# Stick-breaking attention in a two-block transformer kernel: one item per head becomes one item per pair of heads

## The chip, the cores and the metric

The kernel runs on one core of one Trainium2 chip. The metric is device time in microseconds, the median of three runs. PE is the tensor engine (matmuls; PEld are its weight loads), DVE the vector engine, ACT the scalar engine, POOL GpSimd, SP the queue that issues most of the DMAs. Each engine works through its own instructions in the order in which the program issued them.

## The reference

Two transformer blocks on 512 tokens of width 1024. The first block has two layers, and each layer mixes an attention of one kind (NSA) with stick-breaking attention; the change touches the stick-breaking attention only, so it is run twice (layer 0 and layer 1).

```python
def stick_breaking_attention(q, k, v):            # 8 heads of 64, blocks of 128
    for i in range(T // SB_QBLOCK):
        z = einsum(q[q0:q1], k[:q1]) * scale
        strict = k_pos < q_pos
        log_1m = where(strict, -softplus(z), 0.0)
        later = cumsum(log_1m, reverse=True) - log_1m
        w = where(strict, exp(log_sigmoid(z) + later), 0.0)
        out = einsum(w, v[:q1])
```

In `hybrid_mixer` the result goes on as `y = g_a * (o_nsa @ w_proj_nsa) + g_b * (o_sb @ w_proj_sb)`.

## The kernel before

**The stage.** `sb_attn` keeps keys on the partitions and queries on the free axis. An item is one head and one block `j` of 128 keys, with the `512 - 128 j` queries that may see it, so 128 to 512 columns. There are 32 items a layer. Per item:

- PE computes the scores into one PSUM bank: one fp32 matmul with 64 contracted rows (L1190), which the machine runs as two passes, and one small matmul that adds the mask (L1191). Even heads lie on partitions 0 to 63, odd heads on 64 to 127.
- DVE clips them (L1195), ACT takes the exponential and then ln(1+x) (L1196, L1197), DVE takes the maximum with the scores (L1201): this is softplus. ACT rounds it into the high part (L1202), DVE subtracts it for the low part (L1206).
- PE adds the sums over the later keys to the scores, with a matrix of minus ones over each later key block (L1214) and a triangle for the block itself (L1216), each for the high and the low part. Block 3 is padded to 256 columns with zeros.
- ACT takes the exponential, the weights (L1217). PE multiplies them by the values into an output bank (L1224; fp32 again, 64 output rows, a head's half of the partitions). After a pair's last item ACT and DVE split that bank into high and low part (L231, L232).

**The order.** It is written by hand as a software pipeline: iteration `t` computes scores of item `t`, softplus of `t` and `t-1`, the sums and the weights of `t-2`, and every second iteration the outputs of `t-4` and `t-3`. `self.fill(0.6)` puts other work between: `merge_a`, the NSA projection, cut into 32 steps of three matmuls of 512 columns (L223 to L225). Eight steps use one weight unit; every four steps end in two DVE instructions (L729, L730) that empty the PSUM bank. Four banks hold scores, two hold outputs, two the filler.

**The weights.** `Weights` has four slots of a high and a low tile. ACT rounds a unit into the high tile (L112), POOL (here) or DVE subtracts for the low one (L121). `nsa_in` borrows two of the four slots for NSA's keys (`K4`), and `nsa_attn` brings them back at its end. After `sb_attn` comes `merge_out`, whose first matmuls (L223 with `Hh`) take the next PSUM bank in turn.

Of the kernel before, what the change touches and what calls it, by code (L numbers as in the profile page):

```python
# [16 lines left out]
T = 512  # L17
# [156 lines left out]
class Net:  # L174
# [633 lines left out]
    def mix1(self, l):  # L808
        tc = self.tc
        pool = lambda st, name, side: st.enter_context(tc.tile_pool(name=name, bufs=1, side=side))  # L810
        with ExitStack() as st:
            O = pool(st, "oA", "left")
            oA = (O.tile([128, 4, T], F32R, name="oAh"), O.tile([128, 4, T], F32R, name="oAl"))
            tA = O.tile([128, 8, T], F32, name="tA")
            with ExitStack() as sb:
                S = pool(sb, "sv", "right")
                sv = S.tile([128, 4, 512], F32, name="sv")
                with ExitStack() as sn:
                    NP = pool(sn, "nsa", "left")
                    qS = NP.tile([128, 8, T], F32R, name="qS")  # L820
                    vN = NP.tile([128, 4, 2, 128], F32, name="vN")
                    vc = NP.tile([128, 2, 4, 64], F32, name="vc")
                    gt = NP.tile([128, 4, 24], F32, name="gt")
                    gcm = NP.tile([128, 4, 8], F32, name="gcm")
                    kl1 = NP.tile([128, 1024], F32R, name="kl1")
                    with ExitStack() as s2:
                        K4 = self.nsa_in(l, pool(s2, "nsain", "left"), qS, vN, vc, gt, gcm, kl1, sv, tA)
                    S = pool(sb, "sqk", "right")
                    sq = S.tile([128, 4, T], F32, name="sq")
                    sk = S.tile([128, 4, T], F32, name="sk")  # L830
                    with ExitStack() as s2:
                        self.nsa_attn(pool(s2, "nsaat", "left"), qS, K4, vN, vc, gt, gcm, kl1, oA, sq, sk, tA)
                O = pool(st, "oB", "left")
                oB = (O.tile([128, 4, T], F32R, name="oBh"), O.tile([128, 4, T], F32R, name="oBl"))
                with ExitStack() as s2:
                    self.sb_attn(pool(s2, "sbat", "left"), sq, sk, sv, oB, self.merge_a(oA, tA))
            self.merge_out(st, 4, oB, tA, self.a["g_post_mix"][l], self.a["g_pre_ffn"][l])

    def nsa_in(self, l, R, qS, vN, vc, gt, gcm, kl1, sv, tA):
# [18 lines left out]
        def rope(ps, i, nh, out):  # L858
# [142 lines left out]
    def nsa_attn(self, R, qS, K4, vN, vc, gt, gcm, kl1, oA, sq, sk, tA):  # L1001
        nc, PS = self.nc, self.PS
        mm = nc.tensor.matmul
# [21 lines left out]
        items = [(i, kv * 4 + g) for i in range(4) for g in range(4) for kv in range(2)]  # L1025
        n = len(items)
# [131 lines left out]
        self.drain()  # L1158
        self.W.flush()
        self.W.defer, self.W.lo = False, nc.vector  # L1160
        self.W.bring_back()

    def sb_attn(self, R, sq, sk, sv, oB, fill):
        nc, PS = self.nc, self.PS
        mm = nc.tensor.matmul
        A = [h[:, e * T:e * T + T] for h in self.hn for e in range(2)]
        NZ = 4
        self.banks = [6, 7]
        Wt = [h[:, e * T:e * T + T] for h in (self.gpost, self.gpre) for e in range(2)]
        nb = {0: 1, 1: 2, 2: 2, 3: 2}  # L1170
        SP = {j: [R.tile([128, 2, max(256, T - 128 * j)], F32R, name=f"sp{j}_{i}") for i in range(nb[j])] for j in range(4)}
        for t in SP[3]:
            nc.vector.memset(t[:, :, 0:128].bitcast(F32), 0.0)
        items = [(0, 3), (0, 2)]
        for h in range(7):
            items += [(h, 1), (h + 1, 3), (h, 0), (h + 1, 2)]
        items += [(7, 1), (7, 0)]
        n = len(items)

        def part_of(t):  # L1180
            h, j = items[t]
            N = T - 128 * j
            o = 128 if j == 3 else 0
            return h, j, N, PS[:, t % NZ, :N], A[t % 4][:, :N], SP[j][h % nb[j]][:, :, o:o + N]

        def st_z(t):
            h, j, N, z, a, _ = part_of(t)
            p, e = divmod(h, 2)
            r = slice(64 * e, 64 * e + 64)
            mm(z, sk[r, p, j * 128:j * 128 + 128], sq[r, p, j * 128:], start=True, stop=False)  # L1190
            mm(z[:, 0:128], self.identb, self.sbmaskb, start=False, stop=True)  # L1191

        def st_exp(t):
            h, j, N, z, a, _ = part_of(t)
            nc.vector.tensor_scalar(a, z, 40.0, None, op0=OP.min)  # L1195
            nc.scalar.activation(a, a, AF.Exp)  # L1196
            nc.scalar.activation(a, a, AF.Ln, bias=1.0)  # L1197

        def st_sp(t):
            h, j, N, z, a, sp = part_of(t)  # L1200
            nc.vector.tensor_max(a, a, z)  # L1201
            nc.scalar.activation(sp[:, 0], a, AF.Copy)  # L1202

        def st_lo(t):
            h, j, N, z, a, sp = part_of(t)
            nc.vector.tensor_sub(sp[:, 1], a, sp[:, 0].bitcast(F32))  # L1206

        def st_c(t):
            h, j, N, z, _, sp = part_of(t)
            for j2 in range(3, j, -1):  # L1210
                s2 = SP[j2][h % nb[j2]]
                c0 = (min(j2, 2) - j) * 128
                for e in range(2):
                    mm(z[:, c0:], self.nones, s2[:, e], start=False, stop=False, skip_group_check=True)  # L1214
            for e in range(2):
                mm(z, self.ntri, sp[:, e], start=False, stop=e == 1, skip_group_check=True)  # L1216
            nc.scalar.activation(Wt[t % 4][:, :N], z, AF.Exp)  # L1217

        def st_e(ts):
            for t in ts:  # L1220
                h, j = items[t]
                p, e = divmod(h, 2)
                O = PS[:, NZ + p % 2, :]
                mm(O[64 * e:64 * e + 64, j * 128:], sv[:, j, h * 64:h * 64 + 64], Wt[t % 4][:, :T - 128 * j],  # L1224
                   start=j == 3, stop=j == 0, skip_group_check=True)
                if j == 0 and e == 1:
                    self.split2(oB[0][:, p], oB[1][:, p], O)
# [20 lines left out]
        self.W.defer, self.W.lo = False, nc.vector  # L1248


    def reg_mix2(self):
# [472 lines left out]
```

## Time and profile before

| | |
|---|---|
| median of three runs | 2891.37 us (2890.51 to 2892.0) |
| profiled execution | 2889.35 us, its span 2887.4 us |
| PE busy | 2832.1 us (98%) |
| DVE, ACT, POOL busy | 1416.8 us (49%), 1128.5 us (39%), 370.5 us (13%) |
| granted clock of PE, mean share of full speed | 0.994 |

Busy time is the time in which an engine has an instruction under way. Matmuls overlap in the pipeline, so a matmul's own duration is longer than what it adds: that is the distance from its start to the start of the next one.

### The profile page before, as it was taken

Reading aid. Unit: us, or ns where it says so; the run is one execution under the profiler, and the core shown is the slowest. Engines: PE = TensorE matmul, PEld = TensorE weight load, DVE = VectorE, ACT = ScalarE, POOL = GpSimd, SP = SyncE. Lnnn points to the kernel's source line nnn. Section 1 sums busy time; section 2 is a strip of 40 time slices with the busy share of each in tenths; the row PEclk is TensorE's granted clock in tenths of the full one; section 3 lists DMA queues with packets and bytes.
Section 4 is the critical chain, followed back from the end, with each engine's and each line's share of the span. In section 5 each row is a group of like instructions: output and inputs, shape, how many; then the busy total and the mean of one; then the engine's idle time right before and its main releaser. Section 6 shows DMA issues by size and latency. Waiting matters only on the chain.

```text
span 2887.4 us, 34979 instructions
## 1 busy us (share of the span) xinstructions
PE 2832.1 (98%) x14228; PEld 2290.7 (79%) x14228; DVE 1416.8 (49%) x2248; ACT 1128.5 (39%) x2046; POOL 370.5 (13%) x287
## 2 busy tenths in 40 slices
PE   8999999999999999999999999999999999999998
PEld 7777578888878786688888888888776978888887
DVE  5666645544555566545535453233653343533334
ACT  3444634433433445534424342222444232432222
POOL 5221100100122221101101020000522010000000
PEclk9999999999999999999999999999999999999999
DMA  4111123333322111132323322322331222322322
GB/s 156 63 59 30 37 95 100 109 122 93 96 97 90 59 37 45 52 131 76 110 99 99 116 88 88 101 96 95 127 98 61 77 77 95 110 88 95 102 90 78
DMA packets 234322, 255.48 MB, mean 88 GB/s; under 512 B 33073, under 2 KB 193185, under 8 KB 233777
## 3 DMA queue, kind: packets, MB, share of 16 engines
q1 hardware_dynamic: 228016, 233.53, 25.3%
q0 software_dynamic: 4992, 16.94, 1.9%
q10 hardware_dynamic: 1152, 2.77, 0.3%
q8 instruction: 111, 1.82, 0.3%
q14 instruction: 51, 0.41, 0.0%
HBM read 248.60 MB, written 5.53 MB: 88 GB/s over the span
## 4 chain that ended last, share of the span: by engine, by line
PE 92%; DVE 5%; ACT 2%; issue 1%; DMA 0%; DVEq 0%; SPq 0%; ACTq 0%
PE PS L223 25%; PE PS L225 25%; PE PS L224 25%; PE PS L422 2%; PE PS L1190 2%; DVE x L585 2%; PE PS L1124 1%; PE PS L1110 1%; PE PS L1080 1%; PE PS L425 1%; PE PS L1224 1%; PE PS L460 1%; PE PS L1214 1%; PE PS L1216 1%; DVE hn L339 1%
## 5 line engine op out<-in xcount | busy, mean ns | idle before, releaser
L121 DVE TENSOR_TENSOR wlo<-wraw,whi 128x1024 fp32r<-128x1024 f32 (+3 forms) x364 | 437.1, 1206 | 730.3 <-ACT whi L112 730.2
L223 PE MATMUL PS<-Hh,whi 128*128 128x512 f32 x1952 | 776.1, 398 | 1.2 <-DVE nak L1358 0.2
L225 PE MATMUL PS<-Hh,wlo 128*128 128x512 f32 x1952 | 761.1, 390 | 0.2 <-DVE wlo L121 0.2
L224 PE MATMUL PS<-Hl,whi 128*128 128x512 f32 x1952 | 760.5, 390 | 0.0
L112 ACT ACTIVATE whi<-wraw 128x1024 fp32r<-128x1024 f32 (+2 forms) x432 | 436.9, 1016 | 341.6 <-PE PS L225 280.5
L223 PEld LDWEIGHTS PS<-Hh,whi 128*128 128x128 f32 x1952 | 366.6, 188 | 85.2 <-issue 10.3
L225 PEld LDWEIGHTS PS<-Hh,wlo 128*128 128x128 f32 x1952 | 366.4, 188 | 78.2 <-DVE wlo L121 0.8
L224 PEld LDWEIGHTS PS<-Hl,whi 128*128 128x128 f32 x1952 | 367.0, 188 | 70.7
L121 POOL TENSOR_TENSOR wlo<-wraw,whi 128x1024 fp32r<-128x1024 f32 (+1 forms) x68 | 168.2, 2475 | 1304.5 <-ACT whi L112 1304.5
L223 PE MATMUL PS<-whi,gh 128*128 128x512 f32 x624 | 242.9, 389 | 0.0
L225 PE MATMUL PS<-whi,gl 128*128 128x512 f32 x624 | 242.8, 389 | 0.0
L224 PE MATMUL PS<-wlo,gh 128*128 128x512 f32 x624 | 242.7, 389 | 0.0
L231 ACT ACTIVATE gh<-gg 128x512 fp32r<-128x512 f32 x88 | 55.6, 632 | 327.1 <-DVE gg L643 178.9
L223 PEld LDWEIGHTS PS<-whi,gh 128*128 128x128 f32 x624 | 117.4, 188 | 24.5
L224 PEld LDWEIGHTS PS<-wlo,gh 128*128 128x128 f32 x624 | 117.3, 188 | 24.5
L225 PEld LDWEIGHTS PS<-whi,gl 128*128 128x128 f32 x624 | 117.1, 188 | 24.1
L641 POOL TENSOR_TENSOR gg<-cg,cu 128x512 f32<-128x512 f32 x44 | 56.7, 1288 | 549.5 <-DVE cu L624 549.5
L232 DVE TENSOR_TENSOR gl<-gg,gh 128x512 fp32r<-128x512 f32 x88 | 60.9, 693 | 125.5 <-ACT gh L231 125.5
L223 PE MATMUL PS<-whi,Hh 128*128 128x512 f32 (+2 forms) x320 | 118.4, 370 | 2.4 <-ACT whi L112 2.2
L224 PE MATMUL PS<-wlo,Hh 128*128 128x512 f32 (+2 forms) x320 | 116.7, 365 | 0.5 <-DVE wlo L121 0.5
L225 PE MATMUL PS<-whi,Hl 128*128 128x512 f32 (+2 forms) x320 | 116.0, 363 | 0.1
L1091 DVE TENSOR_REDUCE small<-PS 128x2 f32<-128x256 f32 (+3 forms) x64 | 52.7, 824 | 72.0 <-PE PS L1082 61.1
(340 smaller groups left out, 4082.7 us busy)
## 6 DMA issues: line engine op xcount, KB each, us to landing
wraw<-in_w_in_dram SPq DMA_DIRECT2D x56, 1024.0 KB, 5.0
wraw<-in_w_up_dram SPq DMA_DIRECT2D x40, 1024.0 KB, 5.1
wraw<-in_ffn_w_gate_dram SPq DMA_DIRECT2D x20, 1024.0 KB, 5.2
wraw<-in_ffn_w_up_dram SPq DMA_DIRECT2D x20, 1024.0 KB, 5.2
wraw<-in_w_down_dram SPq DMA_DIRECT2D x16, 1024.0 KB, 5.0
wraw<-in_ffn_w_down_dram SPq DMA_DIRECT2D x16, 1024.0 KB, 5.1
wraw<-in_w_out_dram SPq DMA_DIRECT2D x12, 1024.0 KB, 4.9
wraw<-in_w_down_dram SPq DMA_DIRECT2D x8, 768.0 KB, 4.3
```

The lines of the kernel that those rows point to most:

```text
L112: self.nc.scalar.activation(hi, raw, AF.Copy)
L121: self.lo.tensor_sub(lo, raw, hi.bitcast(F32))
L223: mm(out, lh, rh, start=start, stop=False)
L224: mm(out, lh, rl, start=False, stop=False)
L225: mm(out, ll, rh, start=False, stop=stop)
L231: nc.scalar.activation(hi, src, AF.Copy)
L232: nc.vector.tensor_sub(lo, src, hi.bitcast(F32))
L422: self.nc.tensor.matmul(ps[:, sl], ww[:, k], self.Hh[:, k, sl], start=k == 0 and ww is w[0], stop=False)
L585: nc.vector.scalar_tensor_tensor(x, f, r, x, op0=OP.mult, op1=OP.add)
L641: nc.gpsimd.tensor_mul(g, cg[j % 3], cu[j % 3])
L1091: nc.vector.reduce_max(m, S2, axis=AX.X, negate=True)
L1190: mm(z, sk[r, p, j * 128:j * 128 + 128], sq[r, p, j * 128:], start=True, stop=False)
```

## The change

An item becomes a key block of a **pair** of heads, with the two heads in two neighbouring PSUM banks, and each DVE and ACT step is one instruction over both. Key blocks 2 and 3 are one item of 256 + 128 columns, so a pair has three items (2, then 1, then 0) of 2 x 384, 2 x 384 and 2 x 512 columns, and a layer has 12 items in 15 iterations. Three items hold six banks; outputs have one bank (6), the filler one (7). The softplus of block 0, and of every second pair that of block 1, lies in the two borrowed weight slots, which come back only at the end of `sb_attn`. Within an iteration ACT now has `ln` of item `t` behind the weights of `t-2`, and outputs are made for item `t-3` in every iteration. The filler gives a fixed number of steps: four in the first two iterations, two in each later one. The padding of block 3 is gone. The first line of the diff stands at the end of `nsa_attn`.

```diff
-        self.W.bring_back()
...
-    def sb_attn(self, R, sq, sk, sv, oB, fill):
+    def sb_attn(self, R, sq, sk, sv, oB, K4, fill):
...
+        pair = lambda v: v.rearrange("p (e n) -> p e n", e=2)
+        A = [pair(h) for h in self.hn]
+        Wt = [pair(self.gpost), pair(self.gpre)]
+        K4 = [pair(t) for t in K4]
+        self.banks = [7]
+        O = PS[:, 6, :]
+        sp = lambda n, m: [R.tile([128, 2, m], F32R, name=f"{n}{e}") for e in range(2)]
+        SP = {0: [K4[0:2]] * 2, 1: [sp("spb", 384), K4[2:4]], 2: [sp(f"spa{i}", 384) for i in range(2)]}
+        items = [(p, j) for p in range(4) for j in (2, 1, 0)]
...
+            s = 2 * (t % 3)
+            return p, j, PS[:, s:s + 2, :N], A[t % 2][:, :, :N], [v[:, :, :N] for v in SP[j][p % 2]]
 
         def st_z(t):
-            h, j, N, z, a, _ = part_of(t)
-            p, e = divmod(h, 2)
-            r = slice(64 * e, 64 * e + 64)
-            mm(z, sk[r, p, j * 128:j * 128 + 128], sq[r, p, j * 128:], start=True, stop=False)
-            mm(z[:, 0:128], self.identb, self.sbmaskb, start=False, stop=True)
...
+            for jj in (2, 3) if j == 2 else (j,):
+                c = 256 if jj == 3 else 0
+                for e in range(2):
+                    r = slice(64 * e, 64 * e + 64)
+                    mm(z[:, e, c:c + T - 128 * jj], sk[r, p, jj * 128:jj * 128 + 128], sq[r, p, jj * 128:], start=c == 0, stop=False)
...
+        def st_min(t):
+            _, _, z, a, _ = part_of(t)
             nc.vector.tensor_scalar(a, z, 40.0, None, op0=OP.min)
             nc.scalar.activation(a, a, AF.Exp)
+
+        def st_ln(t):
+            a = part_of(t)[3]
             nc.scalar.activation(a, a, AF.Ln, bias=1.0)
...
+            sa, sb = SP[2][p % 2], SP[1][p % 2]
+            later(128 * (3 - j), sa, 256, 384)
+            if j < 2:
+                later(128 * (2 - j), sa, 0, 256)
+            if j == 0:
+                later(128, sb, 0, 384)
+            for i, u in enumerate(s):
+                mm(z[:, e], self.ntri, u[:, e], start=False, stop=i == 1, skip_group_check=True)
...
             if 0 <= t - 1 < n:
                 st_sp(t - 1)
             if t < n:
-                st_exp(t)
+                st_min(t)
             if 0 <= t - 1 < n:
                 st_lo(t - 1)
             if 0 <= t - 2 < n:
-                st_c(t - 2)
-            self.fill(0.6)
-            if t >= 4 and t % 2 == 0:
-                st_e((t - 4, t - 3))
+                st_c(t - 2, 0)
+                st_c(t - 2, 1)
+                st_w(t - 2)
+            if t < n:
+                st_ln(t)
+            steps(4 if t < 2 else 2)
+            if 0 <= t - 3 < n:
+                st_e(t - 3)
```

In the changed file the scores are L1192 and the masks L1195, `min` is L1199, `exp` L1200, `ln` L1204, `max` L1208, the rounding L1209, the low part L1213, ones and triangle L1220 and L1229, the weights L1233, the outputs L1241.

**PE inside the stage.** Before, in the second head's turn: outputs of two items (`gpre` holds the weights, `sv` the values), then the scores of one head (`sq`, `sk`), its mask, sums (`sp`), one filler step, and the next head's scores.

```order
L1224 MATMUL PS<-gpre,sv 64x384
L1224 MATMUL PS<-gpre,sv 64x128
L1190 MATMUL PS<-sq,sk 128x128
L1191 LDWEIGHTS identb
L1191 MATMUL PS<-sbmaskb,identb 128x128
L1214 MATMUL PS<-sp_1_2276,nones 128x256 x2
L1216 MATMUL PS<-sp_1_2274,ntri 128x256 x2
L223 MATMUL PS<-oAh,whi_66 128x512
L224 MATMUL PS<-oAl,whi_66 128x512
L225 MATMUL PS<-oAh,wlo_67 128x512
L1190 MATMUL PS<-sq,sk 128x512
```

Now, in iteration 4, the outputs of both heads, then the scores of both heads, both masks, and the first head's sums (`spa` is the softplus of blocks 2 and 3, `spb` that of block 1).

```order
L1241 MATMUL PS<-gpost,sv 64x256 x2
L1192 MATMUL PS<-sq,sk 128x384 x2
L1195 LDWEIGHTS identb
L1195 MATMUL PS<-sbmaskb,identb 128x128
L1195 LDWEIGHTS identb
L1195 MATMUL PS<-sbmaskb,identb 128x128
L1220 MATMUL PS<-spa_2272,nones 128x128
L1220 MATMUL PS<-spa_2273,nones 128x128
L1220 MATMUL PS<-spa_2272,nones 128x256
L1220 MATMUL PS<-spa_2273,nones 128x256
L1220 MATMUL PS<-spb_2270,nones 128x384
L1220 MATMUL PS<-spb_2271,nones 128x384
```

The score matmuls of the even and the odd head now stand side by side, as do the two output matmuls of equal width.

**ACT inside the stage.** Before, with `hn` the work tile and `gpre`, `gpost` the weights:

```order
L1202 ACTIVATE sp_1_2276<-hn_78 128x128
L1196 ACTIVATE hn_77<-hn_77 128x512
L1197 ACTIVATE hn_77<-hn_77 128x512
L1217 ACTIVATE gpre<-PS 128x384
L1202 ACTIVATE sp_0_2270<-hn_77 128x512
L1196 ACTIVATE hn_77<-hn_77 128x256
```

Now, from the rounding in iteration 5 to the pair's output split:

```order
L1209 ACTIVATE whi_70<-hn_77 128x2x384
L1200 ACTIVATE hn_78<-hn_78 128x1024
L1233 ACTIVATE gpre<-PS 128x2x384
L1204 ACTIVATE hn_78<-hn_78 128x1024
L231 ACTIVATE oBh<-PS 128x512
```

The `ln` has moved behind the weights of the item two before, and the split of the output bank stands behind it.

**PE at the end of the stage.** Before, with what each waits for, the last sums, the last filler step, the last outputs, and the first matmul of `merge_out` (`Hh`):

```order
L1216 MATMUL PS<-sp_0_2270,ntri 128x512 [waits DVE_49]
L223 MATMUL PS<-oAh,whi_70 128x512
L224 MATMUL PS<-oAl,whi_70 128x512
L225 MATMUL PS<-oAh,wlo_71 128x512
L1224 MATMUL PS<-gpre,sv 64x384 [waits Activation_49]
L1224 MATMUL PS<-gpre,sv 64x512 [waits Activation_49]
L223 MATMUL PS<-Hh,whi_66 128x512
```

Now:

```order
L1241 MATMUL PS<-gpost,sv 64x384 [waits Activation_49]
L1241 MATMUL PS<-gpost,sv 64x384
L1241 MATMUL PS<-gpre,sv 64x512 [waits Activation_49]
L1241 MATMUL PS<-gpre,sv 64x512
L223 MATMUL PS<-Hh,whi_66 128x512 [waits DVE_49]
L224 MATMUL PS<-Hl,whi_66 128x512
```

The first matmul of `merge_out` now waits for DVE: its bank in turn is 6, which held the outputs that DVE's L232 reads last.

## Rows read from the trace of the kernel before

**Rows 1.** Busy time by stretch: the stage in both layers.

The columns are the stretch, its length, busy time and instructions of PE, PEld, DVE, ACT and POOL, granted clock, DMA share, GB/s.

```profile
277.00:369.00 92.00, 91.08 (x419) 51.49 (x417) 60.62 (x118) 62.43 (x138) 10.56 (x5) 1.00 0.09 30
1114.00:1206.00 92.00, 91.20 (x417) 51.83 (x418) 60.70 (x119) 62.54 (x139) 11.41 (x5) 1.00 0.09 29
```

**Rows 2.** All waits of PE in layer 0's stage, 277.11 to 369.

```profile
PE PS L223 <- DVE oAl L232: 0.8, 1, 0.8
```

**Rows 3.** Timeline of PE in that stage: start, duration, instruction, count.

```profile
283.00 0.48 PE L1190 MATMUL PS<-sq,sk 64*128 64x128 f32 x2
283.42 0.23 PE L1191 MATMUL PS<-sbmaskb,identb 128*128 128x128 bf16 x1
...
284.25 0.39 PE L224 MATMUL PS<-oAl,whi 128*128 128x512 f32 x1
284.48 0.39 PE L225 MATMUL PS<-oAh,wlo 128*128 128x512 f32 x1
284.79 1.12 PE L1190 MATMUL PS<-sq,sk 64*128 64x512 f32 x2
285.85 0.23 PE L1191 MATMUL PS<-sbmaskb,identb 128*128 128x128 bf16 x1
...
288.38 0.70 PE L1190 MATMUL PS<-sq,sk 64*128 64x256 f32 x2
289.01 0.23 PE L1191 MATMUL PS<-sbmaskb,identb 128*128 128x128 bf16 x1
...
293.19 0.86 PE L1224 MATMUL PS<-gpre,sv 128*64 128x384 f32 x4
293.98 0.48 PE L1190 MATMUL PS<-sq,sk 64*128 64x128 f32 x2
...
364.16 1.07 PE L1224 MATMUL PS<-gpost,sv 128*64 128x512 f32 x4
365.16 1.09 PE L1214 MATMUL PS<-sp,nones 128*128 128x256 f32 x6
```

**Rows 4.** Timeline of PE in the second block: two heads' scores side by side.

```profile
2181.39 0.70 PE L1481 MATMUL PS<-hn,hn 64*128 64x256 f32 x4
2182.02 0.50 PE L223 MATMUL PS<-Hh,whi 128*128 128x512 f32 x1
```

**Rows 5.** Groups by line and shape, whole run: busy us, mean ns of one.

```profile
L112 ACT ACTIVATE whi<-wraw 128x1024 fp32r<-128x1024 f32 x392 | 410.0, 1050 | 282.9 <-PE PS L225 236.0 <-issue 18.9 <-DMA wraw<-in_w_in_dram 9.7
L112 ACT ACTIVATE whi<-wraw 128x768 fp32r<-128x768 f32 x8 | 6.7, 842 | 0.1
L1091 DVE TENSOR_REDUCE small<-PS 128x2 f32<-128x1024 f32 x16 | 19.6, 1225 | 24.5 <-PE PS L1082 24.5
L1091 DVE TENSOR_REDUCE small<-PS 128x2 f32<-128x768 f32 x16 | 15.3, 958 | 18.6 <-PE PS L1082 18.6
L1206 DVE TENSOR_TENSOR sp<-hn,sp 128x256 fp32r<-128x256 f32 x16 | 17.3, 1080 | 2.3 <-ACT sp L1202 2.1
```

**Rows 6.** Timeline of all engines: a hand-over, and the end of the stage.

```profile
282.13 0.56 DVE L1195 TENSOR_SCALAR hn<-PS 128x384 f32<-128x384 f32 x1
...
282.73 0.52 ACT L1196 ACTIVATE hn<-hn 128x384 f32<-128x384 f32 x1
...
368.99 0.50 PE L223 MATMUL PS<-Hh,whi 128*128 128x512 f32 x1
369.10 0.60 ACT L231 ACTIVATE oBh<-PS 128x512 fp32r<-128x512 f32 x1 [0.80 <-PE PS L1224]
...
369.73 0.69 DVE L232 TENSOR_TENSOR oBl<-PS,oBh 128x512 fp32r<-128x512 f32 x1 [1.59 <-ACT oBh L231]
```

**Rows 7.** Busy time by stretch elsewhere: PE with gaps, and its granted clock.

```profile
2254.30:2257.80 3.50, 2.93 (x21) 2.51 (x21) 2.20 (x11) 2.40 (x12) 0.00 (x0) 1.00 0.26 90
2257.80:2261.30 3.50, 3.50 (x17) 3.28 (x16) 1.85 (x11) 3.10 (x15) 0.36 (x1) 0.51 0.00 0
2330.00:2344.00 14.00, 11.08 (x78) 6.48 (x74) 9.43 (x26) 4.15 (x7) 2.04 (x2) 1.00 0.24 75
```

More of the change, by code (lines that the diff above doesn't have):

```diff
@@ L835, in mix1 @@
                 with ExitStack() as s2:
-                    self.sb_attn(pool(s2, "sbat", "left"), sq, sk, sv, oB, self.merge_a(oA, tA))
+                    self.sb_attn(pool(s2, "sbat", "left"), sq, sk, sv, oB, K4, self.merge_a(oA, tA))
             self.merge_out(st, 4, oB, tA, self.a["g_post_mix"][l], self.a["g_pre_ffn"][l])
@@ L1160, in nsa_attn @@
         self.W.defer, self.W.lo = False, nc.vector
-        self.W.bring_back()
-    def sb_attn(self, R, sq, sk, sv, oB, fill):
+    def sb_attn(self, R, sq, sk, sv, oB, K4, fill):
         nc, PS = self.nc, self.PS
         mm = nc.tensor.matmul
[L1166 to L1177, printed above, removed]
+        pair = lambda v: v.rearrange("p (e n) -> p e n", e=2)
[7 more added lines that the diff above has]
+        items = [(p, j) for p in range(4) for j in (2, 1, 0)]
@@ L1178, in sb_attn @@
         n = len(items)
+        NJ = {0: 512, 1: 384, 2: 384}
         def part_of(t):
[L1181 to L1184, printed above, removed]
+            p, j = items[t]
+            N = NJ[j]
+            s = 2 * (t % 3)
+            return p, j, PS[:, s:s + 2, :N], A[t % 2][:, :, :N], [v[:, :, :N] for v in SP[j][p % 2]]
         def st_z(t):
-            h, j, N, z, a, _ = part_of(t)
@@ L1188, in st_z @@
-            p, e = divmod(h, 2)
-            r = slice(64 * e, 64 * e + 64)
-            mm(z, sk[r, p, j * 128:j * 128 + 128], sq[r, p, j * 128:], start=True, stop=False)
-            mm(z[:, 0:128], self.identb, self.sbmaskb, start=False, stop=True)
-        def st_exp(t):
-            h, j, N, z, a, _ = part_of(t)
+            p, j, z, _, _ = part_of(t)
+            for jj in (2, 3) if j == 2 else (j,):
[3 more added lines that the diff above has]
+                    mm(z[:, e, c:c + T - 128 * jj], sk[r, p, jj * 128:jj * 128 + 128], sq[r, p, jj * 128:], start=c == 0, stop=False)
@@ L1195, in st_exp @@
+            for c in (0, 256) if j == 2 else (0,):
+                for e in range(2):
+                    mm(z[:, e, c:c + 128], self.identb, self.sbmaskb, start=False, stop=c == 256 or j < 2)
+        def st_min(t):
+            _, _, z, a, _ = part_of(t)
             nc.vector.tensor_scalar(a, z, 40.0, None, op0=OP.min)
             nc.scalar.activation(a, a, AF.Exp)
+        def st_ln(t):
+            a = part_of(t)[3]
             nc.scalar.activation(a, a, AF.Ln, bias=1.0)
         def st_sp(t):
-            h, j, N, z, a, sp = part_of(t)
+            _, _, z, a, s = part_of(t)
@@ L1201, in st_sp @@
             nc.vector.tensor_max(a, a, z)
-            nc.scalar.activation(sp[:, 0], a, AF.Copy)
+            nc.scalar.activation(s[0], a, AF.Copy)
         def st_lo(t):
[L1205 to L1212, printed above, removed]
-                for e in range(2):
[L1214 to L1227, printed above, removed]
+            _, _, _, a, s = part_of(t)
+            nc.vector.tensor_sub(s[1], a, s[0].bitcast(F32))
@@ new lines, in st_c, with later @@
+        def st_c(t, e):
+            p, j, z, _, s = part_of(t)
+            def later(c, v, c0, c1):
+                for u in v:
+                    mm(z[:, e, c:c + c1 - c0], self.nones, u[:, e, c0:c1], start=False, stop=False, skip_group_check=True)
+            sa, sb = SP[2][p % 2], SP[1][p % 2]
[6 more added lines that the diff above has]
+                mm(z[:, e], self.ntri, u[:, e], start=False, stop=i == 1, skip_group_check=True)
@@ new lines, in st_w, with st_e @@
+        def st_w(t):
+            p, j, z, _, _ = part_of(t)
+            nc.scalar.activation(Wt[t % 2][:, :, :NJ[j]], z, AF.Exp)
+        def st_e(t):
+            p, j = items[t]
+            for jj in (3, 2) if j == 2 else (j,):
+                c = 256 if jj == 3 else 0
+                for e in range(2):
+                    h = 2 * p + e
+                    mm(O[64 * e:64 * e + 64, jj * 128:], sv[:, jj, h * 64:h * 64 + 64], Wt[t % 2][:, e, c:c + T - 128 * jj],
+                       start=jj == 3, stop=jj == 0, skip_group_check=True)
+            if j == 0:
+                self.split2(oB[0][:, p], oB[1][:, p], O)
@@ L1229, in sb_attn, with steps @@
+        def steps(k):
+            self.W.flush()
+            while k and self.fillq:
+                if next(self.fillq[0], None) is None:
+                    self.fillq.pop(0)
+                else:
+                    k -= 1
         self.table(LN_EXP_SET)
@@ L1248, in sb_attn @@
         self.W.defer, self.W.lo = False, nc.vector
+        self.W.bring_back()
     def reg_mix2(self):
```

## The prediction, written before the changed kernel ran

> **What bounds the kernel now.** I read the busy times by stretch first, because the change touches only two stretches. In both the tensor engine is busy for 91.1 and 91.2 of 92 us at the full clock, while DVE and ACT are busy for about two thirds [rows 1]. The view of waits then shows that PE waits only once in layer 0's stage, 0.8 us at its start [rows 2]. So the stage is as long as the sum of PE's distances from one start to the next, and what DVE and ACT do in it is hidden. Shortening DVE or ACT work gains nothing by itself; what counts is what PE no longer streams, and then whether DVE and ACT can follow the faster PE.
>
> **What PE saves, per pair of heads.** I count distances from start to start on PE's timeline.
>
> *Scores.* One head's matmul of 128 columns takes 283.00 to 283.42, 0.42 us; of 256, 0.63; of 512, 1.06 [rows 3]. The 384 wide one lies half way between the last two, 0.84. One head costs 0.42 + 0.63 + 0.84 + 1.06 = 2.95, a pair 5.90 today. In the second block the scores of an even and an odd head already stand side by side, 256 columns each, and the four passes of both take 2181.39 to 2182.02, 0.63 us [rows 4]: as much as one head alone. The lower and the upper half of the array work at the same time. The change puts them side by side for every width, so a pair should cost 2.95 and **save 2.95**. The bounds are nothing (no overlap) and 2.95; I take the row with the same form.
>
> *Outputs.* A 384 wide matmul beside a 128 wide one takes 0.79 us, a 512 wide beside a 256 wide one 1.00 [rows 3]. A pair has two of each, 3.58. Now the two heads' matmuls have equal widths. For 512 with 512 I take 1.00, for 384 with 384 0.79, since today's time already is about that of the wider one; for the item of 128 and 256 columns no row exists, and it lies between 0.79 and 1.00: 0.89. Sum 2.68, **saved 0.90**.
>
> *Changes of the array's shape.* From the last filler matmul to the scores PE needs 0.31 us (284.48 to 284.79) against 0.23 between filler matmuls (284.25 to 284.48) [rows 3]. Eight groups of scores and four of outputs a pair become three and three: six times 0.08, **saved 0.5**.
>
> *Masks and sums.* There are eight mask matmuls a pair before and after, 0.23 long each in the pipeline [rows 3], but they now stand in runs. That may cost nothing or up to 8 x 0.23; they are short and their weights the same, so I let it lose 0.1. The sums need 36 matmuls a pair instead of 40, since the triangle covers blocks 2 and 3 at once; some get wider, six get narrower. I price this at nothing; at the most it saves 4 x 0.23 = 0.9.
>
> Together 2.95 + 0.90 + 0.5 - 0.1 = 4.25 us a pair, 17.0 us a layer. PE alone would need 92 - 17 = **75.0 us** a stage.
>
> **Whether DVE and ACT can follow.** They have fewer instructions, but each is longer, and they form a chain, because only three items are under way and each engine takes its work in order. From `ln` of item t-1: DVE takes the maximum, then clips item t while ACT rounds; ACT takes `exp` of t, the weights of t-2, `ln` of t. The prices are those of 1024 and 768 columns: ACT 1.05 and 0.84, DVE 1.23 and 0.96 [rows 5], the DVE ones being reads of PSUM like these. A hand-over costs 282.73 - (282.13 + 0.56) = 0.04 us [rows 6], about 0.2 an iteration.
>
> - Key block 2 follows block 0: 1.23 + 1.05 (rounding, longer than clipping at 0.96) + 0.84 + 0.84 + 0.84 + 0.2 = 5.0.
> - Block 1: 0.96 + 0.96 + 0.84 + 1.05 + 0.84 + 0.2 = 4.85.
> - Block 0: 0.96 + 1.23 + 1.05 + 0.84 + 1.05 + 0.2 = 5.33.
>
> That is 15.2 a pair. Once a pair the output split gets in: PE comes to the outputs only after two filler steps (6 x 0.23 = 1.4) and the outputs themselves (1.0), then ACT copies in 0.60 and DVE subtracts in 0.69 [rows 6], so DVE is free 3.7 us after the sums, where `ln` would have released it after 0.84 + 1.05 = 1.9. The next maximum is 1.8 late. Three such holds lie inside the stage. Four pairs are 60.8, the holds 5.4, and a tail follows the last `ln`: maximum 1.23, rounding 1.05, low part 1.23, the second head's nine sum matmuls (1.6 at 0.18), weights 1.05, outputs 1.0, hand-overs 0.2 = 7.4. The chain alone needs **73.6 us**.
>
> **The end of the stage.** The first matmul of `merge_out` now waits for the split of the outputs, since its bank in turn is the output bank. Before, that split ran beside it: 368.99 to 369.73 + 0.69 = 370.42 [rows 6]. This **costs 1.4 us** a layer.
>
> **What costs nothing.** With two weight slots instead of four only one unit is split ahead. The filler takes a unit every four iterations, some 20 us, and a split needs 1.05 on ACT [rows 5] and then POOL, all beside that; the first gate unit of `merge_out` (24 x 0.23 = 5.5 us) covers the second's. Uncovered it would be 1.05 and a DVE copy of 1.2, 2.3 us a layer. The DMAs are the same ones, later by a few us.
>
> **The sum.** PE alone gives 75.0, the chain alone 73.6. Two lines so equal wait for each other in turn, since scores of item t need the bank that the weights of t-3 release; I add 0.1 us for each of the 15 iterations, a choice between nothing and the 0.8 that PE's one wait had. Stage 75.0 + 1.5 + 1.4 = 78 at the most, 75.0 + 1.4 = 76.4 at the least. I take **77**, 15 us less a layer, 30 in all. The profiled execution took 2889.35 us, its span 2887.4; 30 less is 2859.4, and the median of the runs lay 2.0 above that execution: **2861 us**.
>
> **The rivals.** A change within 0.2% (5.8 us) could hardly be told from none.
>
> *DVE and ACT become the bound outright.* When POOL works on a weight unit, DVE's low parts stretch: those of 256 columns took 1080 ns on average [rows 5], where a clip of 384 columns takes 0.56 [rows 6]. POOL does five units in a stage, 11.41 / 5 = 2.3 us each [rows 1]. If each delayed the chain by its whole copy and the holds were doubled, the chain would be 73.6 + 11.5 + 5.4 = 90.5 and 1.4, with nothing saved; half of that gives 82 + 1.4 a stage, 8.6 saved, about 2874. Against it: after clipping, DVE has 2.7 us until the next maximum and needs 1.2 for the low part, so 1.5 of each stretch is free. Beside this stands the Trainium skill, TensorEngine Tiling (Array Packing), section Performance Considerations: packing speeds up TensorE but not the emptying of PSUM, which may become the bottleneck. By it the outcome is this rival. Chance of 2871 to 2885: 0.14.
>
> *The two heads' scores do not overlap.* Then 11.8 of the 17.0 go, PE needs 86.8 + 1.4, and the time is 2884 to 2888. The pairs in the second block speak against it. Chance 0.04.
>
> *Nothing that can be told,* for instance because weights come late after the stage and give the gain back: 0.03, and half of the last rival falls here too.
>
> *Slower: PE's clock falls.* PE will wait a little in every iteration. Elsewhere a stretch with PE busy for 2.93 of 3.5 us was followed by one at a granted clock of 0.51, 1.2 GHz; another with 11.08 of 14 stayed at 1.00 [rows 7]. In a stretch at half clock PE does half of its work. The 30 us are eaten up when 60 us of the two stages, of some 154, run at half; if all did, PE would need 150 a stage, and the time would be about 3010. The rows show both answers; the gaps expected here are short ones. The Trainium skill, TensorE: Matmul & The Clock Gate, section HAM oscillation, describes a loop in which waits between groups of matmuls take the clock down in each round; by it this rival would come true if the waits were long. Two or three such stretches would cost 1.7 us each and stay in my range. Chance of slower: 0.04.
>
> *Better than forecast.* If the sums save their 0.9 a pair (PE 71.4) and the holds vanish because PE reaches the outputs early (chain 68.2), the stage is 71.4 + 1.4, and the time 2853; about there and below: 0.07.
>
> **Numbers.** The forecast itself, 2852 to 2871, has 0.68. The range 2850 to 2876 takes in part of the first rival and leaves out about 2 in 10. Faster by over 0.2%: 0.91; within: 0.05; slower: 0.04.
>
> **What would show it.** In the profile after, the stage from the first scores to the first `Hh` matmul of `merge_out` should take 75 to 79 us in both layers; two heads' scores of 512 columns should take some 1.06 us from their start to the mask, and start some 10 ns apart; PE's waits in the stage should sum to 3 to 6 us, with the weights (ACT) and the low parts (DVE) as releasers; the first matmul of `merge_out` should wait 1.4 us for DVE's low output; ACT's instructions should follow each other with little idle time. I am wrong if the scores of a pair take twice 1.06, if one iteration takes 6 us or more throughout, if the stretches show a granted clock near 0.5, or if PE waits for weights in `merge_out`.

## The result and the profile after

The changed kernel takes **2851.35 us**, the median of four runs (2850.97 to 2853.08), beside 2891.59 us (2890.51 to 2892.0) for the kernel before: a ratio of 0.9863 with a 95% interval of 0.9845 to 0.988, 40.2 us less. The forecast was 2861, its range 2850 to 2876; the mechanism held, and its larger terms were too small. The profiled execution took 2851.37 us, its span is 2849.4, against 2889.35 and 2887.4 before.

The stage from the first scores to the first `Hh` matmul of `merge_out` is the view to begin with, as in [rows 1]: length, busy time and instructions of PE, PEld, DVE, ACT and POOL, granted clock, DMA share, GB/s.

```profile
279.67:351.88 72.21, 69.55 (x401) 47.26 (x401) 50.10 (x57) 49.71 (x59) 9.28 (x4) 1.00 0.07 23
1093.55:1165.78 72.23, 69.56 (x401) 47.26 (x401) 50.11 (x57) 49.71 (x59) 9.29 (x4) 1.00 0.07 23
```

Cut in the same way, the stage before took 91.88 and 91.89 us. Each layer lost 19.7, both 39.3; the span lost 38.0, so everything else together became 1.3 longer. More than that lies ahead of the first stage, in code that is the same in both: the stage starts at 279.67 instead of 277.11, and the granted clock was 0.83 instead of 0.89 in the first 30 us and 0.77 instead of 0.89 from 95 to 110. In the rows above, PE is still busy for 69.6 of 72.2 us at the full clock. DVE and ACT have half their instructions (57 and 59 instead of 118 and 138), but only about a fifth less time. PE's waits in layer 0, where [rows 2] had one of 0.8 (us in total, times, longest):

```profile
PE PS L223 <- DVE oBl L232: 1.4, 1, 1.4
PE PS L1192 <- ACT gpost L1233: 1.0, 2, 0.7
PE PS L1192 <- ACT gpre L1233: 0.3, 1, 0.3
```

PE's timeline around key block 0 of the second pair answers to [rows 3]:

```profile
302.56 0.87 PE L1241 MATMUL PS<-gpre,sv 128*64 128x384 f32 x4
303.35 1.13 PE L1192 MATMUL PS<-sq,sk 64*128 64x512 f32 x4
304.42 0.28 PE L1195 MATMUL PS<-sbmaskb,identb 128*128 128x128 bf16 x2
304.51 0.42 PE L1220 MATMUL PS<-spa,nones 128*128 128x128 f32 x2
304.76 0.56 PE L1229 MATMUL PS<-spa,ntri 128*128 128x384 f32 x2
...
307.22 1.08 PE L1241 MATMUL PS<-gpost,sv 128*64 128x512 f32 x4
308.23 0.92 PE L1192 MATMUL PS<-sq,sk 64*128 64x256 f32 x8
```

The four passes of two heads' scores of 512 columns take 303.35 to 304.42, 1.07 us, as one head alone took before; single starts show the two heads 6 to 7 ns apart. The output matmuls now all go in pairs of equal width, 1.01 us for 512 columns (307.22 to 308.23).

The end of the stage, all engines, as in [rows 6]:

```profile
350.51 0.60 ACT L231 ACTIVATE oBh<-PS 128x512 fp32r<-128x512 f32 x1 [0.78 <-PE PS L1241]
...
351.14 0.69 DVE L232 TENSOR_TENSOR oBl<-PS,oBh 128x512 fp32r<-128x512 f32 x1 [1.60 <-ACT oBh L231]
...
351.88 0.50 PE L223 MATMUL PS<-Hh,whi 128*128 128x512 f32 x1 [1.42 <-DVE oBl L232]
```

**Where PE's time went.** I added the distances from each matmul's start to the next over layer 0's stage, by the kind of the first; a wait counts to the kind ahead of it (of the changed kernel's waits for weights, the longest to the filler, two to the outputs). The columns are us, first the two kernels, then the experiments told below.

```
kernel               scores  masks   sums  filler  outputs  stage
before                23.54   2.27  25.66   25.43    14.98  91.88
after                 11.06   1.58  22.48   24.67    12.42  72.21
scores apart          21.97   2.83  22.47   24.22    11.76  83.25
halves                11.44   1.58  22.31   24.04    11.79  71.15
ACT extra             11.06   1.58  25.18   25.35    16.46  79.65
lighter PE            11.06   1.58  17.61   24.71    14.93  69.89
other bank            11.06   1.58  22.48   24.67    10.93  70.73
sums in old shapes    11.06   1.58  23.33   24.54    11.89  72.41
some halves + bank    11.06   1.59  22.32   24.39    10.27  69.62
```

### The profile page after: what moved, and what is told of

Read it like the earlier page. It is cut to its first block, busy times and chain, and to the rows that moved or that the text cites. A ratio compares the mean times of both kernels' runs of the same rounds, so it can differ in the third digit from the quotient of the medians.

```text
span 2849.4 us, 34641 instructions
## 1 busy us (share of the span) xinstructions
PE 2790.2 (98%) x14196; PEld 2282.4 (80%) x14196; DVE 1397.4 (49%) x2126; ACT 1102.0 (39%) x1886; POOL 365.3 (13%) x285
## 4 chain that ended last, share of the span: by engine, by line
PE 90%; DVE 5%; ACT 3%; issue 1%; DMA 0%; DVEq 0%; ACTq 0%; POOL 0%; POOLq 0%
PE PS L223 26%; PE PS L225 25%; PE PS L224 25%; PE PS L422 2%; DVE x L585 2%; PE PS L1124 1%; PE PS L1110 1%; PE PS L1080 1%; PE PS L425 1%; PE PS L460 1%; DVE hn L339 1%; PE PS L1220 1%; PE PS L1192 1%; PE PS L380 1%; PE PS L1511 1%
## 5 line engine op out<-in xcount | busy, mean ns | idle before, releaser
L232 DVE TENSOR_TENSOR gl<-gg,gh 128x512 fp32r<-128x512 f32 x88 | 60.9, 693 | 125.6 <-ACT gh L231 125.6
```

Source lines behind the costliest of these rows:

```text
L232: nc.vector.tensor_sub(lo, src, hi.bitcast(F32))
```

## The experiments

Theory A is that of the prediction: PE sets the stage, and the gain is what it no longer streams, the overlapping scores first. Theory B says that the gain comes from DVE and ACT having fewer and longer instructions, theory C that their chain is the bound now. Each edit is one of the changed kernel.

**Scores apart.** The loop over heads goes to the outside.

```diff
-            for jj in (2, 3) if j == 2 else (j,):
-                for e in range(2):
+            for e in range(2):
+                for jj in (2, 3) if j == 2 else (j,):
                     ...scores of head e, block jj...
-            for c in (0, 256) if j == 2 else (0,):
-                for e in range(2):
+                for c in (0, 256) if j == 2 else (0,):
                     ...mask of head e...
```

> The changed kernel, but the scores and masks of the first head are issued before those of the second, so that the two heads' scores no longer stand side by side; all else is as in the changed kernel. Theory A, the tensor engine (PE) sets the stage and the overlap of the scores is the largest part of the gain: the scores' distances go from 11.1 us a layer back to about 23.5, and each item has one more passage from the 16 bit masks to 32 bit matmuls; PE's waits of 2.7 us vanish. The stage goes from 72.2 to 82 to 85 us in each layer, the whole from 2851 to 2871 to 2877. Theory B, the gain comes from DVE and ACT having half as many instructions, each twice as long: their instructions are unchanged here, so the stage stays within 2 us of 72.2 and the time below 2856. Theory C, the chain of DVE and ACT has become the bound by itself, clearly above PE: the later scores lengthen only the start of each item, and the stage grows by less than half of 12 us, below 78.

It took 2874.16 us (2871.95 to 2876.76; ratio to before 0.9945, 0.993 to 0.996), its stage 83.25 us in both layers: 11.0 more a layer, as A says. Windows, then PE's timeline of the 512 wide scores:

```profile
277.03:360.28 83.25, 81.31 (x402) 52.46 (x401) 48.92 (x57) 49.95 (x59) 9.24 (x4) 1.00 0.06 20
```
```profile
305.18 1.12 PE L1192 MATMUL PS<-sq,sk 64*128 64x512 f32 x2
306.24 0.23 PE L1194 MATMUL PS<-sbmaskb,identb 128*128 128x128 bf16 x1
306.39 1.12 PE L1192 MATMUL PS<-sq,sk 64*128 64x512 f32 x2
307.45 0.23 PE L1194 MATMUL PS<-sbmaskb,identb 128*128 128x128 bf16 x1
```

The second head starts 1.21 us after the first instead of 7 ns, while DVE and ACT do the same work. The order of one loop gives back more than half of what the whole change won. PE's waits did not vanish as expected under A: 1.4 us for the output bank and 0.5 for weights are left.

**Halves.** Each step of DVE and ACT is two instructions, for instance

```diff
-            nc.vector.tensor_max(a, a, z)
-            nc.scalar.activation(s[0], a, AF.Copy)
+            for e in range(2):
+                nc.vector.tensor_max(a[:, e], a[:, e], z[:, e])
+            for e in range(2):
+                nc.scalar.activation(s[0][:, e], a[:, e], AF.Copy)
```

> The changed kernel, but each step of DVE and ACT on an item (clip, exp, ln, maximum, rounding, low part, weights) is two instructions, one for each head, in the same order; PE's instructions are as in the changed kernel. Theory A: PE sets the stage and DVE and ACT have 22 of 72 us free, so that more and shorter instructions cost little: stage 71 to 75 us, whole 2849 to 2857. Theory B, the gain comes from the longer instructions: DVE and ACT fall back to the number of instructions of before, more than 100 each in a stage, and most of the 19.7 us are given back: stage 84 to 92, whole 2875 to 2891. Theory C, the chain is the bound: it either grows by the instructions' fixed parts, about 0.1 us for each of the 7 x 12 added ones, some 4 to 8 us a layer, or shrinks because the second engine can start on the first half, so the stage moves by several us either way.

2851.75 us (2846.67 to 2852.25), by time the same as the changed kernel; the profiled execution is the fastest of the four, at a mean granted clock of 0.997. What the edit does is read from the stage. DVE has 93 instructions in the stage and ACT 107, and the stage is not longer but 1.06 us shorter, 71.15. Windows and PE's waits:

```profile
275.94:347.09 71.15, 69.55 (x401) 47.62 (x400) 52.67 (x93) 54.15 (x107) 9.30 (x4) 1.00 0.07 24
```
```profile
PE PS L223 <- DVE oBl L232: 1.5, 1, 1.5
PE PS L1192 <- ACT gpost L1240: 0.2, 1, 0.2
```

B falls: that each instruction covers both heads is not where the gain is. What the halves win is PE's waits for weights, 1.3 us in the changed kernel and 0.2 here.

**One more ACT instruction an item.**

```diff
             nc.scalar.activation(a, a, AF.Ln, bias=1.0)
+            nc.scalar.activation(a, a, AF.Copy)
```

> The changed kernel with one added ACT instruction an item behind ln: a copy of the item's values onto themselves, 768 or 1024 columns, about 0.7 and 0.95 us, 2.4 us a pair, 9.5 us a layer. It lies in the chain of DVE and ACT, between ln and the next maximum. Theory C, the chain is the bound and PE follows it: the stage grows by nearly all of it, 8 to 10 us, to 80 to 82, whole 2867 to 2871. Theory A, PE sets the stage and the chain lies clearly below it (by 2.4 us a pair or more): the stage grows by less than 1.5 us, whole below 2855. My own estimate lies between: from the starts of successive ACT and DVE instructions in the changed kernel (0.95 and 0.71 on ACT, 1.13 and 0.87 on DVE) the chain of a pair is about 1 us below the period of 16.1, so that some 1.4 us of each 2.4 come through: 5 to 6 us a layer, stage 77 to 78, whole about 2862.

2868.47 us (2866.04 to 2868.69), stage 79.64 in both layers, 7.4 more: between A and C, and above my 5 to 6. Part of that is not the chain. The table of stretches shows a fall of the granted clock in the second half of the stage:

```profile
313.25:316.65 3.40, 1.61 (x12) 0.74 (x13) 2.56 (x3) 2.90 (x4) 0.00 (x0) 1.00 0.02 5
316.65:320.05 3.40, 3.40 (x23) 2.73 (x20) 2.12 (x3) 3.28 (x5) 1.17 (x1) 1.00 0.00 0
...
330.25:333.65 3.40, 1.96 (x14) 1.01 (x12) 3.15 (x4) 2.21 (x3) 0.00 (x0) 1.00 0.00 0
333.65:337.05 3.40, 3.07 (x14) 2.34 (x15) 2.61 (x5) 2.35 (x4) 0.00 (x0) 0.75 0.00 0
337.05:340.45 3.40, 3.40 (x15) 2.91 (x13) 1.30 (x2) 2.34 (x4) 0.00 (x0) 0.75 0.00 0
340.45:343.85 3.40, 3.40 (x20) 1.90 (x20) 1.87 (x2) 3.26 (x4) 0.88 (x1) 1.00 0.02 5
```

The stretch from 335.34 to 338.75 by itself shows 0.50, 1.2 GHz, and layer 1's stage has another such fall. The period of three items is 17.69 us ahead of it and 19.24 across it, 1.55 more; without that the stage would be some 5.9 longer, of 9.5 added. In the periods the chain lets 17.69 - 16.10 = 1.6 of the added 2.4 us a pair through. So in the changed kernel it lies about 0.8 us a pair below the period, at 15.3. PE's waits here:

```profile
PE PS L1192 <- ACT gpost L1234: 3.2, 2, 1.8
PE PS L1192 <- ACT gpre L1234: 2.5, 2, 1.8
PE PS L223 <- DVE oBl L232: 1.4, 1, 1.4
PE PS L1230 <- DVE wlo L1214: 0.8, 1, 0.8
```

**A lighter PE.**

```diff
-                for u in v:
+                for u in v[:1]:
                     mm(z[:, e, c:c + c1 - c0], self.nones, u[:, e, c0:c1], ...)
```

> The changed kernel without the sums of the later blocks' low parts: of each pair of matmuls with the matrix of minus ones only that with the high part stays, so the values computed lack those low parts. That leaves out 12 matmuls a pair, 48 a layer, some 0.10 to 0.18 us each, about 6.4 us a layer; DVE and ACT do the same work as before. Theory A, PE sets the stage and the chain is well below: stage 72.2 - 6.4 = 66 us, whole about 2839. Theory C, the chain is the bound: the stage stays at 71.5 to 72.2 and the whole above 2849; the prediction on record priced the chain alone at 73.6 with full durations, which would say the same. In between: PE shortens until the chain stops it, and the stage then is the chain's own length; by the starts of successive instructions I expect 68 to 70 us, whole 2843 to 2847. The granted clock in the stage tells besides whether PE with waits of several us keeps 1.00.

2847.89 us (2846.32 to 2848.17), stage 69.89. The sums fell by 4.9 us (22.48 to 17.61), and by 5.9 without a wait for a low part that stands among them and costs 1.0; I had estimated 6.4. The stage fell only by 2.3. Windows and waits:

```profile
278.91:348.80 69.89, 63.96 (x353) 41.40 (x352) 50.45 (x57) 49.55 (x59) 9.30 (x4) 1.00 0.08 24
```
```profile
PE PS L1192 <- ACT gpost L1233: 2.5, 4, 1.2
PE PS L223 <- DVE oBl L232: 1.4, 1, 1.4
PE PS L1192 <- ACT gpre L1233: 1.2, 1, 1.2
PE PS L1229 <- DVE wlo L1213: 0.8, 1, 0.8
```

PE now waits 5.9 us, and the clock stays at 1.00. The chain with whole instructions needs at most 69.9 less the 1.4 at the end, 68.5 us, with a period of 15.7 a pair: by this bound hardly less than PE's 69.6 in the changed kernel. The expectation of 68 to 70 came out.

**The lighter PE with halves.** The same line in the last kernel below.

> The kernel with some halves and the other bank, and besides without the sums of the later blocks' low parts (as in the lighter kernel, so those parts are missing from the values). There PE became 4.9 us lighter a layer (sums 17.6 instead of 22.5 us), but the stage lost only 2.3 and stayed at 69.9, 68.4 without the 1.5 at the end. If whole instructions of DVE and ACT held it there, the halves let it go on down: stage 64.5 to 66.5, that is 69.6 less most of the 4.9. If it was held by something that the halves leave as it is (ACT's total work of about 50 us and its waits, POOL's copies beside DVE, the turn of the three items), the stage is 67 to 68.5.

2841.29 us in its one run, stage 65.75, in the window of the first answer. That is 2.6 below the 68.4 that the lighter PE had without the 1.5 at the end, so the whole instructions had held the stage for the most part. Not for all of it: the sums are 6.0 us lighter than in the last kernel, 3.9 came through, and PE still waits 2.4 us for weights.

```profile
279.03:344.79 65.76, 63.34 (x354) 41.37 (x353) 51.52 (x92) 50.55 (x81) 7.83 (x4) 1.00 0.08 26
```

**The other bank.**

```diff
         self.W.bring_back()
+        self.bi += 1
```

> The changed kernel with one line behind the stage: the turn of the PSUM banks is moved on by one, so that the first matmul of the merge that follows goes to another bank than the one in which the last pair's outputs still wait to be split. Theory: the 1.4 us wait for DVE's low output at the end of each stage is nothing but the turn of the banks. Then that wait is gone, the stage is 70.7 to 70.9 us in both layers, and the whole 2.8 to 3.0 us shorter, about 2848.4. Rival: something else holds PE there just as long (the operands in `Hh`, or the weights): the stage stays at 72.2 and the wait has another releaser. Second rival: a later matmul pays for it, because the turn of the banks then meets another one that is not free: the stage is shorter, the time is not.

Stage 70.73 and 70.72, 1.5 less a layer, and 2849.29 us (2848.29 to 2849.86; ratio to before 0.9855, 0.9838 to 0.9871). PE's waits from 273 to 440, well behind the stage:

```profile
PE PS L1192 <- ACT gpost L1233: 1.0, 2, 0.7
PE PS L1110 <- ACT hn L1115: 0.3, 1, 0.3
PE PS L1192 <- ACT gpre L1233: 0.3, 1, 0.3
```

The wait is gone and none has taken its place: it was the turn of the banks and nothing else. By time alone the 2 to 3 us can't be told from the changed kernel with certainty, since the intervals overlap; the stage tells it.

**Sums in their old shapes.**

```diff
-            later(128 * (3 - j), sa, 256, 384)
+            later(128 * (2 - j), sa, 128, 384)
...
-            for i, u in enumerate(s):
-                mm(z[:, e], self.ntri, u[:, e], ...)
+            for c0, c1 in ((0, 256), (256, 384)) if j == 2 else ((0, NJ[j]),):
+                for i, u in enumerate(s):
+                    mm(z[:, e, c0:c1], self.ntri, u[:, e, c0:c1], ...)
```

> The changed kernel with the sums in the shapes of the kernel before: the triangle's matmuls of blocks 2 and 3 are two instead of one (256 and 128 columns instead of 384, four more matmuls a pair), and the matmuls with block 3's values are 256 columns wide again instead of 128. In this kernel the added 128 columns hold block 2's values instead of zeros, so sums of other columns change. All groups of sums stay joined, two heads behind each other. The sums took 25.7 us a layer before and 22.5 after. Theory S, the shapes make the difference: the sums go back by about 3 us a layer, stage 74.5 to 75.5, whole 2856 to 2858. Theory G, most of it comes from there being 12 groups of sums instead of 23, since the first matmul behind a mask stands 0.20 us from the next instead of 0.12 before, and 0.143 instead of 0.101 after: the shapes give back only about 1 us, stage 72.8 to 73.5, whole 2852.5 to 2854.

2852.06 us (2849.63 to 2854.01). The sums took 23.33 us instead of 22.48: the shapes are worth 0.85 of the 3.18, which speaks for theory G. All of it is at the ones (L1220), 13.53 us here and 12.58 in the changed kernel; the triangles take 9.79 and 9.89. The stage however is only 0.2 longer, 72.41, below both expectations: PE's waits for weights fell from 1.3 to 0.4, so most of the longer sums fitted into time that PE had waited.

**The best version.** The other bank, and halves for the clip, exp, maximum, rounding and low part; ln and the weights stay whole. Two kernels ran first: one with all steps in halves, and this one.

> Two edits together: the steps of DVE and ACT in two instructions, one a head, and the other bank behind the stage. If the two gains are apart (1.06 us a layer by the halves' stage of 71.16, and 1.4 to 1.5 by the bank), the stage is 69.7 us, and the whole 5.0 us less than the changed kernel, about 2846.3. If the tail that the halves shorten and the wait at the end are the same time, the stage is 70.5 to 71.2 and the whole 2848 to 2849.

> As the kernel with both edits, but ln and the weights stay one instruction for both heads; the clip, exp, maximum, rounding and low part are in halves. The halves pay where the second engine can begin on the first head while the first engine is at the second; at ln and the weights ACT waits for nobody's half. If that is so, this saves 24 ACT instructions a layer and is as short as with all halves or up to 0.5 us shorter a layer: stage 69.2 to 69.7, whole 2845.3 to 2846.3. Rival: the halves pay because PE's next scores can follow the first half of the weights; then the stage is longer than with all halves, 70 to 71, whole 2847 to 2849. If PE alone sets the stage by now, both are 69.5 to 69.7.

They took 2846.99 us (2846.06 to 2847.54; ratio 0.9847, 0.9832 to 0.9862) and 2846.83 (2846.42 to 2847.34; 0.9847, 0.9832 to 0.9861), stages 69.64 and 69.62. The gains add up. That both are equal, with PE waiting 0.2 and 0.5 us, says that PE alone sets the stage by then; that the scores wait for half of the weights, the rival, would have made the second one longer. Beside the changed kernel on one chip:

> The changed kernel once more, on the same chip as the next one, to compare the two by time: 2851 us, within 2, stage 72.2.

> The kernel with some halves and the other bank once more beside the changed kernel: by the stages (69.6 instead of 72.2 us) it is 5.2 us shorter, so about 2846; if clock falls elsewhere in the program take part of this back, the difference is smaller than 5.2, and the traces show them outside the two stages.

The changed kernel took 2854.09 us (2851.92 to 2855.19; ratio 0.9873, 0.9856 to 0.9889), the best version 2846.44 (2846.11 to 2846.82; 0.9845, 0.983 to 0.986), stages 72.18 and 69.62. The two layers give 5.1 of the 7.7 us between the medians; the profiled runs of the two lie 5.8 apart. The ranges of the runs don't meet; the intervals of the ratios overlap by a little. Windows of the best version, and PE's waits:

```profile
277.85:347.46 69.61, 69.14 (x401) 47.31 (x400) 51.35 (x92) 51.09 (x81) 7.79 (x4) 1.00 0.08 24
```
```profile
PE PS L1192 <- ACT gpost L1238: 0.5, 1, 0.5
```

## Why the prediction was right, and where its sizes were off

The step that carried it, the overlap of the scores, was right and is shown by the loop order. The terms, in us a layer as I put them and as the table gives them:

| term | predicted | measured |
|---|---|---|
| scores overlap | 11.8 | 12.5 |
| outputs | 3.6 | 4.7 |
| changes of shape, seen at the filler | 2.0 | 1.7 |
| masks | -0.4 | -0.3 |
| wait at the stage's start [rows 2] | 0 | 0.8 |
| sums | 0 | 3.2 |
| wait for the output bank | -1.4 | -1.5 |
| waits for weights (coupling) | -0.6 | -1.4 |
| stage | -15 | -19.7 |

Each wait is taken out of the kind that it counts to, as the excess over the usual distance. The outputs after hold 1.49 for the bank (by the run with the other bank) and 2 x 0.33 for weights: 14.98 - (12.42 - 1.49 - 0.66) = 4.7. The filler after holds the third wait for weights, 0.78, and 0.19 that is left of the wait at the start: 25.43 - (24.67 - 0.78 - 0.19) = 1.7. The masks before hold 1.02, the whole wait at the start: 2.27 - 1.02 - 1.58 = -0.3. Only the scores and in part the sums have a run of their own; the other terms are read from distances.

*Scores.* The 128 wide matmuls of block 3 now follow the 256 wide ones of block 2, and both take 0.86 us; I had priced 0.63 + 0.42 = 1.05.

*Sums.* **This is the mis-sized term that cost most.** The text counted matmuls and priced the sums "at nothing; at the most it saves 4 x 0.23 = 0.9" a pair; they saved 0.8. The run with the old shapes gives 0.85 a layer to the shapes (12 matmuls a pair became narrower, not six). For the other 2.3 the starts of single matmuls show three sources. The first matmul of a group, mostly behind a mask, stands 0.20 us from the next where others of 256 columns stand 0.12, and 0.143 where others of 128 stand 0.060 (the 0.101 in the expectation is not what the starts show). There were 23 and 8 such groups a layer and are 12 in all, so 19 x 0.08 = 1.5. Two groups had held PE in the middle for the low parts, 0.6 in sum (362.69 and 303.10). Four groups had scores or outputs behind them and not the filler, 0.4 in sum. That is 2.5, the 2.3 within 0.2. The step missed that fewer groups mean fewer changes on both sides of the sums.

*Outputs and changes of shape.* The outputs gave 1.1 more than priced. The item of blocks 2 and 3 takes 0.80 us and not 0.89, four times a layer; and the last group before, two matmuls of one head from 367.35 to 368.99, had taken 1.64 and not 1.00. The changes of shape were near: from the filler to scores or outputs PE passes 14 times where it passed 29 times, so 15 times fewer at 0.09 us, and not 24 times at 0.08.

*The chain of DVE and ACT*, priced at 73.6 us alone. Too high by at least 5: the lighter PE bounds it at 68.5. I added full durations. ACT's timeline in the changed kernel:

```profile
306.00 1.06 ACT L1200 ACTIVATE hn<-hn 128x1024 f32<-128x1024 f32 x1 [0.91 <-DVE hn L1199]
306.96 0.80 ACT L1233 ACTIVATE gpre<-PS 128x768 f32<-128x768 f32 x1
307.65 1.05 ACT L1204 ACTIVATE hn<-hn 128x1024 f32<-128x1024 f32 x1
308.60 0.59 ACT L231 ACTIVATE oBh<-PS 128x512 fp32r<-128x512 f32 x1
```

An instruction of 1.06 us is followed after 0.96, one of 0.80 after 0.69: about 0.1 each is counted twice. The Trainium skill, Perfetto Trace Analysis, section Optimizing Scalar/DVE Operations, says that part of a profiled latency overlaps with the next instruction; these rows agree, with 0.1 us. The output split holds the next maximum less than the 1.8 that I took. DVE's timeline:

```profile
309.22 0.69 DVE L232 TENSOR_TENSOR oBl<-PS,oBh 128x512 fp32r<-128x512 f32 x1 [1.21 <-ACT oBh L231]
309.83 1.21 DVE L1208 TENSOR_TENSOR hn<-hn,PS 128x1024 f32<-128x1024 f32 x1
...
316.19 2.35 DVE L1213 TENSOR_TENSOR spa<-hn,spa 128x768 fp32r<-128x768 f32 x1
318.47 0.41 DVE L729 TENSOR_SCALAR tA<-tA 128x512 f32<-128x512 f32 x1
318.99 0.69 DVE L730 TENSOR_TENSOR tA<-tA,PS 128x512 f32<-128x512 f32 x1
319.59 0.95 DVE L1208 TENSOR_TENSOR hn<-hn,PS 128x768 f32<-128x768 f32 x1
```

`ln` had ended at 307.65 + 1.05 = 308.70, the maximum begins at 309.83: 1.1.

*Two equal lines wait for each other.* Right in kind: PE alone needs 91.9 - 22.6 = 69.3, the chain at most 68.5, the stage without its end 70.7, and both the extra ACT instruction and the lighter PE come through in part. Of the two signs that I named, the weights were seen as releasers, the low parts only with the lighter PE and the extra ACT instruction. That the two lines stayed equal is luck: each was priced over 5 us too high. With PE as it came out and the chain at its 73.6, the stage with its end would have been 75.0 and not 72.2.

*The end of the stage* was right (1.4 predicted, 1.4 seen, 1.5 taken away by the other bank), and so was *what costs nothing*: from the stage's end to 430 us PE waits for nothing but that bank.

**The rivals.** *The chain as the bound* did not come true, but was close, and its mechanism is there: beside POOL's work on a weight unit the low part above took 2.35 us, and with the filler's additions behind it the maximum came at 319.59, 0.45 after `ln`'s end, not the whole 2.3. The rule of the Trainium skill that stood beside it (TensorEngine Tiling (Array Packing), Performance Considerations) is seen half: PE's next 5.9 us bring only 2.3. *No overlap* is refuted. *The falling clock* stayed away from both stages; the extra ACT instruction brought it, with waits of up to 1.8 us, so a chain longer by those 2.4 us a pair would have met the condition. HAM oscillation in the Trainium skill, TensorE: Matmul & The Clock Gate, speaks of falls in each round of a loop; here one of four periods had one. *Better than forecast* is what came: the sums saved nearly all of their 0.9 a pair, though the holds did not vanish, and the time is 1.7 us below that rival's 2853. Its chance of 0.07 was too small for a case that needed only the terms priced at nothing to be worth something.

The time lies 1.4 us above the range's lower end and below the 2852 to 2871 that I gave 0.68. The signs: the stage was to take 75 to 79 and took 72.2; PE's waits 3 to 6 and were 2.7; ACT was to have little idle time, and was busy for 49.7 of 72.2. The forecast lay 9.7 us above the median: 9.3 are the two stages (39.3 instead of 30), 2.0 the added distance from the profiled execution to the median, which the changed kernel did not show; 1.3 go the other way for the rest of the program, and 0.4 was rounded off.

## What to carry to other kernels

When the tensor engine is the bound, look for matmuls that use half of the array and issue two of them directly behind each other, with nothing between: here one loop's order is 11 us of a 72 us stage. Count the changes between kinds of matmuls on both sides of every group, since fewer groups pay even where the columns stay the same. Then size the chain behind it from start to start, and where it comes near the bound, split its instructions where one engine hands over to another; leaving whole those for which nobody waits, `ln` and the weights, made no difference here (69.62 and 69.64 us).

## What the runs showed of the hardware

- The first sum of a group stands 0.20 us from the next behind a 16 bit mask and 0.22 behind outputs, others of 256 columns 0.12; of 128 columns 0.143 and 0.163 against 0.060.
- Narrowing 48 sums a layer from 256 to 128 columns saved 0.95 us, 0.02 each: two of 128 columns stand 0.06 us apart and one 0.11 from a wider one, but the first of 256 behind them 0.17 from the next instead of 0.118.
- With the extra ACT instruction the clock fell at 335.34, behind a wait of 1.8 us that ended at 333.98; a stretch with PE busy for 1.61 of 3.40 us in the same stage was followed by no fall. With the lighter PE it stayed at 1.00 through 5.9 us of waits, of which none but the last was over 1.2.
- DVE's low part of 768 columns takes 0.95 us alone. Begun at 316.19, while POOL subtracted 1024 columns until 317.73, it took 2.35, to 0.8 behind POOL's end.
